# Side pieces wait for a read bank, and two transposes become pieces of their own

## The chip, the cores and the metric

The kernel runs on one core of one Trainium2 chip. The metric is the device time of one launch in microseconds (us): the median of several runs, 1270.43 us for the kernel before (three runs, 1270.27 to 1271.31).

## The reference, cut to what matters

One inference step of a decoder layer, for a prompt of 512 tokens and a sample group of 8 sequences with 4 tokens each (544 token columns in all), everything in float32. Cut down:

```python
u = rmsnorm(h)
qa, ka, va, qkv_b, z_b, beta, a, gate_a, gate_b = split(u @ w_in)
A = dilated_attention(qa, ka, va)     # 3 dilations x 4 heads x 64; the sample reads cached keys and values
B = gated_deltanet(qkv_b, z_b, beta, a)   # 8 heads x 128, convolution ahead, chunked recurrence, matrix state
h += (sigmoid(gate_a) * (A @ w_branch_a) + sigmoid(gate_b) * (B @ w_branch_b)) @ w_out
h += cross_attention(rmsnorm(h), memory)  # 256 memory tokens, 4 heads
h += (silu(conv3(n @ W_gate) + b) * (n @ W_up)) @ W_down,   n = rmsnorm(h)
y = rmsnorm(h)
```

All new caches and states are outputs too. What the change touches is the sample's part of the dilated attention: one softmax per sample row over all three dilations, and the product with the values.

## The kernel before

**Dense work.** The weights come as 128x1024 blocks, in the order of a fixed plan. Each block is loaded (`wr`), split into a high part `wh` (ScalarE copy) and a low part `wl` (VectorE subtraction), and multiplied as three products (high by high, high by low, low by high) with the 544 columns in two halves of 272. So one of the eight steps of a block is six matmuls into a wide PSUM buffer `pd`; two such buffers take turns. `u` is the normed input (`uh`, `ul`), `A` and `ob` the two branches (`Ah`, `obh`, and so on), `m` the memory tokens, `th` a gate.

**Side work.** Everything else (dilated attention, DeltaNet, softmaxes, transposes) runs in between as generators, "streams". A piece is what a stream does between two `yield`s; it usually begins with matmuls or transposes into small PSUM banks `b`, of which there are four in rotation, and ends with VectorE (DVE) or ScalarE (ACT) instructions that read them. Names: `ssc` holds the sample's scores, `so` its output, `kc` cached keys or values, `qz` and `pz` the queries and probabilities spread out, `dk`, `dq`, `sc`, `pt`, `vt` the prompt's dilated attention; `y` convolved rows, `vm` and `sz` the update of the sample's DeltaNet states, `U`, `W`, `T` the inverse of a triangular matrix, `xc`, `vn`, `St` the recurrence over chunks, `ft` and `z` tiles fetched back from DRAM.

**What sets the order.** While the program is built, an account keeps a clock for each engine, by a cost for each instruction. After every dense step `tick` (L635) goes through the streams that are runnable, by priority, and runs a piece if its inputs are ready by the account, memory slots are free, and VectorE and ScalarE do not lag too far behind. The engines then run their instructions in just that order. A piece whose `yield` says `"at", t` is ready at t. The stream `dil_sample` is marked free (`free=True`): what its pieces leave running is not counted for its readiness, only what it names with `on` or `"at"`. `acc.last` holds, for each tile, when the account has its last use done; `slot_of` keeps the list of banks in `self.ring["b"]`; `acc.done` is when the latest instruction of the piece ends. All instructions are recorded through one helper, so every row of the profile has the line L329.

Of the kernel before, what the change touches and what calls it, by code (L numbers as in the profile page):

```python
# [392 lines left out]
class Builder:  # L393
# [239 lines left out]
    def tick(self):  # L633

        c = self.clk  # L635
        t0 = c["PE"]
        self.flush()
        while c["PE"] - t0 < PE_SHARE:
            runs = self.runnable()
            for n in sorted(range(len(runs)), key=lambda n: (runs[n]["prio"], runs[n]["ready"])):  # L640
                st = runs[n]
                lag = max(c["V"], c["A"]) - c["PE"]
                if st["ready"] <= c["PE"] and self.room(st, [a + b for a, b in zip((MAIN, 0), self.older(runs, n))]) and lag < LAG[st["prio"]] and c["P"] - c["PE"] < 6.0:
                    self.step(st)
                    break
            else:
                return
# [1032 lines left out]
    def dil_sample(self):  # L1680
# [64 lines left out]
        n = 0  # L1745
# [41 lines left out]
        v.reciprocal(z, z)  # L1787
        v.tensor_scalar(sc, sc, z, None, op0=OP.mult)
        del bs
        yield 1, 0, 2, 0  # L1790
        pb = self.bank((128, 384))
        for g in range(3):
            nc.tensor.transpose(pb[:, 128 * g:128 * g + 128], sc[:, col(g):col(g) + 128], ident)
# [16 lines left out]
        for g in range(3):  # L1810
            for j in range(8 if g else 2):
# [9 lines left out]
                n += 1  # L1821
                yield
        v.tensor_tensor(o, o, acc[:, None, :].to_broadcast([128, 2, 64]), OP.add)
        yield from self.wait(("ap", 0), ("ap", 1))
        pb = self.bank((128, 128))
        nc.tensor.transpose(pb, o.rearrange("p h d -> p (h d)"), ident)
# [460 lines left out]
MAIN, PE_SHARE, LAG = 5, 2.5, {0: 4.5, 1: 2.0, 2: 2.0, 3: 1.5}  # L2287
# [52 lines left out]
```

## Time and profile before

| | |
|---|---|
| median of 3 runs | 1270.43 us |
| the profiled execution | 1269.83 us |
| its span | 1268.1 us |
| TensorE busy | 1222.2 us (96%) |
| VectorE / ScalarE / GpSimd busy | 709.4 / 526.6 / 160.9 us |
| granted TensorE clock, mean | 0.988 of full speed |

The span is the first to the last instruction; the execution has 1.7 us around it. TensorE's busy time counts overlapping matmuls once and includes slow ones, so stalls show as idle time before an instruction, in brackets with what ended it, and a lower clock shows in the windows.

### The profile page before, as it was taken

How to read it: one execution, taken by the hardware profiler on the slowest of the kernel's cores; microseconds unless marked ns; L12 is line 12 of the kernel's file. 1: busy time of each engine (PE TensorE's matmuls, PEld its weight loads, DVE VectorE, ACT ScalarE, POOL GpSimd, SP SyncE). 2: the span in 40 equal slices, each digit the busy share in tenths (PEclk: the TensorE clock that was granted, in tenths of full speed). 3: DMA queues.
4: the chain of work that ended last, by engine and by line, in shares of the span. 5: the costliest groups of instructions: out<-in, count | busy, mean ns of one | idle time of the engine just before them, and what ended most of it. 6: DMA issues, size and time to landing. Idle time of an engine off the chain costs nothing.

```text
span 1268.1 us, 25946 instructions
## 1 busy us (share of the span) xinstructions
PE 1222.2 (96%) x10482; PEld 1165.2 (92%) x10482; DVE 709.4 (56%) x1343; ACT 526.6 (42%) x1115; POOL 160.9 (13%) x356
## 2 busy tenths in 40 slices
PE   7999999999999999998999999799999999999997
PEld 6899988899999988998799998499999999999997
DVE  6535346666767974486566555364553355434564
ACT  6334434555645533665642234254332233312341
POOL 0000100211152130020000000021210022101110
PEclk9999999999999998999998999899999999999998
DMA  6332774653576568656564483545555555555422
GB/s 224 95 122 79 279 265 155 214 174 100 178 267 215 200 215 295 199 190 193 175 219 143 166 325 110 191 171 186 193 187 183 183 189 206 203 184 183 157 83 71
DMA packets 90117, 233.56 MB, mean 184 GB/s; under 512 B 25865, under 2 KB 31478, under 8 KB 89221
## 3 DMA queue, kind: packets, MB, share of 16 engines
q1 hardware_dynamic: 89998, 231.90, 53.1%
q8 instruction: 83, 1.36, 0.4%
q14 instruction: 36, 0.29, 0.1%
HBM read 198.42 MB, written 77.58 MB: 218 GB/s over the span
## 4 chain that ended last, share of the span: by engine, by line
PE 71%; DVE 5%; ACT 2%; issue 2%; DMA 1%; POOL 0%; DVEq 0%; POOLq 0%; SPq 0%; ACTq 0%
PE pd L329 58%; PE b L329 13%; DVE wl L329 1%; DVE y L329 1%; ACT wh L329 1%; DMA qk<-park 0%; DVE xr L329 0%; DMA ft<-park 0%; DVE sz L329 0%; DVE m L329 0%; DMA mvs<-in_mvs 0%; DVE st L329 0%; DMA z<-park 0%; ACT hsq L329 0%; DVE su L329 0%
## 5 line engine op out<-in xcount | busy, mean ns | idle before, releaser
L329 DVE TENSOR_TENSOR wl<-wr,wh 128x1024 fp32r<-128x1024 f32 (+2 forms) x174 | 212.4, 1223 | 225.2 <-ACT wh L329 219.1
L329 ACT ACTIVATE wh<-wr 128x1024 fp32r<-128x1024 f32 (+2 forms) x174 | 177.1, 1021 | 122.7 <-PE pd L329 120.5
L329 PE MATMUL pd<-uh,wh 128*128 128x272 f32 x1024 | 223.5, 300 | 0.0
L329 PE MATMUL pd<-ul,wh 128*128 128x272 f32 x1024 | 212.7, 289 | 0.4 <-DVE ul L329 0.3
L329 PE MATMUL pd<-uh,wl 128*128 128x272 f32 x1024 | 212.3, 288 | 0.0
L329 PEld LDWEIGHTS pd<-uh,wh 128*128 128x128 f32 x1024 | 160.2, 189 | 7.7 <-issue 6.4
L329 PEld LDWEIGHTS pd<-ul,wh 128*128 128x128 f32 x1024 | 162.1, 189 | 0.9 <-DVE ul L329 0.8
L329 PE MATMUL pd<-nh,wh 128*128 128x272 f32 x768 | 161.6, 291 | 0.5 <-DVE xr L329 0.5
L329 PEld LDWEIGHTS pd<-uh,wl 128*128 128x128 f32 x1024 | 161.8, 188 | 0.0
L329 PE MATMUL pd<-nh,wl 128*128 128x272 f32 x768 | 159.4, 288 | 0.0
L329 PE MATMUL pd<-nl,wh 128*128 128x272 f32 x768 | 159.3, 288 | 0.0
L329 PEld LDWEIGHTS pd<-nh,wh 128*128 128x128 f32 x768 | 121.9, 188 | 2.3 <-issue 2.0
L329 PEld LDWEIGHTS pd<-nl,wh 128*128 128x128 f32 x768 | 121.7, 188 | 0.0
L329 PEld LDWEIGHTS pd<-nh,wl 128*128 128x128 f32 x768 | 121.6, 188 | 0.0
L329 POOL TENSOR_TENSOR sr<-fy,rf 128x512 f32<-128x512 f32 (+1 forms) x44 | 53.5, 1237 | 69.5 <-ACT fy L329 66.3
L329 DVE SCALAR_TENSOR_TENSOR y<-cb,par,y 128x568 f32<-128x568 f32 x72 | 58.9, 820 | 2.9 <-ACT y L329 1.1
L329 PE MATMUL pd<-fh,wh 128*128 128x272 f32 x256 | 53.2, 288 | 0.0
L329 PE MATMUL pd<-fl,wh 128*128 128x272 f32 x256 | 53.1, 288 | 0.0
L329 PE MATMUL pd<-fh,wl 128*128 128x272 f32 x256 | 53.1, 288 | 0.0
L329 DVE SCALAR_TENSOR_TENSOR fy<-fcb,par,fy 128x560 f32<-128x560 f32 x44 | 35.3, 802 | 22.4 <-ACT fy L329 21.7
L329 PEld LDWEIGHTS pd<-fh,wl 128*128 128x128 f32 x256 | 40.6, 188 | 0.0
L329 PEld LDWEIGHTS pd<-fh,wh 128*128 128x128 f32 x256 | 40.5, 188 | 0.0
(371 smaller groups left out, 2121.0 us busy)
## 6 DMA issues: line engine op xcount, KB each, us to landing
wr<-in_w SPq DMA_DIRECT2D x145, 512.0 KB
out_d<-in_c SPq DMA_DIRECT2D x32, 1022.0 KB
ft<-park SPq DMA_DIRECT2D x40, 256.0 KB
kc<-in_ck SPq DMA_DIRECT2D x18, 512.0 KB
kc<-in_cv SPq DMA_DIRECT2D x18, 512.0 KB
wr<-in_wd SPq DMA_DIRECT2D x16, 512.0 KB
out_d<-in_c SPq DMA_DIRECT2D x8, 1016.0 KB
park<-y SPq DMA_DIRECT2D x24, 256.0 KB
```

The source lines that it names most:

```text
L329: return f(*a, **k)
```

## The change

`tick` asks one more thing of a stream before it runs a piece: the bank that is the fourth last in the list, the one the next piece will take first, must have been used for the last time by the account's TensorE clock. In `dil_sample`, the piece with the transposes of `ssc` is no longer ready at once behind the softmax, but when the account has the softmax done; and the final transpose of `so` likewise waits for the last addition.

```diff
-                if st["ready"] <= c["PE"] and self.room(st, [a + b for a, b in zip((MAIN, 0), self.older(runs, n))]) and lag < LAG[st["prio"]] and c["P"] - c["PE"] < 6.0:
+                if max(st["ready"], self.acc.last.get(self.ring["b"][-4], 0.0) - 0.0 if len(self.ring["b"]) >= 4 else 0.0) <= c["PE"] and self.room(st, [a + b for a, b in zip((MAIN, 0), self.older(runs, n))]) and lag < LAG[st["prio"]] and c["P"] - c["PE"] < 6.0:
                     self.step(st)
...
         v.tensor_scalar(sc, sc, z, None, op0=OP.mult)
         del bs
-        yield 1, 0, 2, 0
+        yield "at", self.acc.done, (1, 0, 2, 0)
         pb = self.bank((128, 384))
         for g in range(3):
             nc.tensor.transpose(pb[:, 128 * g:128 * g + 128], sc[:, col(g):col(g) + 128], ident)
...
         v.tensor_tensor(o, o, acc[:, None, :].to_broadcast([128, 2, 64]), OP.add)
+        yield "at", self.acc.done, (0, 0, 0, 0)
         yield from self.wait(("ap", 0), ("ap", 1))
         pb = self.bank((128, 128))
         nc.tensor.transpose(pb, o.rearrange("p h d -> p (h d)"), ident)
```

Every engine has the same number of instructions as before; their order differs from the dilated attention of the prompt (about 180 us) to the end of the branch products (about 674 us). Numbers in the rows below are buffer numbers and differ between the two programs.

TensorE before, around the transposes of the softmax's result (`ssc`): a product of the prompt's attention (`pt`, `vt`) ends, one dense step follows, then the transposes.

```order
L329 MATMUL b_2439<-pt_2412,vt_1923 64x128
L329 MATMUL b_2439<-pt_2423,vt_1923 64x128
L329 MATMUL pd_2343<-uh_409,wh_2153 128x272 x2
L329 MATMUL pd_2343<-ul_410,wh_2153 128x272 x2
L329 MATMUL pd_2343<-uh_409,wl_2154 128x272 x2
L329 MATMUL b_2466<-ident,ssc_274 128x128 x3
L329 MATMUL b_2487<-dk_1014,dq_924 128x512
```

TensorE now at the same transposes (the end of 24 rows of dense matmuls, eight steps):

```order
L329 MATMUL pd_2515<-uh_409,wh_2339 128x272 x2
L329 MATMUL pd_2515<-ul_410,wh_2339 128x272 x2
L329 MATMUL pd_2515<-uh_409,wl_2340 128x272 x2
L329 MATMUL pd_2515<-uh_419,wh_2339 128x272 x2
L329 MATMUL pd_2515<-ul_420,wh_2339 128x272 x2
L329 MATMUL pd_2515<-uh_419,wl_2340 128x272 x2
L329 MATMUL b_2566<-ident,ssc_274 128x128 x3
```

The transposes moved nine dense steps down. The final transpose of `so`, once behind a product of `kc` and `pz`, now has three dense steps between.

ScalarE before, at the first block of the memory keys and values: `m<-sso` is the root for a pair of heads, with a table load on each side of it, `th` the last gate, `wh_7786` and `wh_7828` weights of the memory blocks.

```order
L329 ACTIVATE ft_7144<-b_7753,rqs_4235 128x128
L329 ACT_TABLE_LOAD
L329 ACTIVATE m_7773<-sso_5305,eps 128x4x2
L329 ACT_TABLE_LOAD
L329 ACTIVATE th_7777<-pd_7689 128x544
L329 ACTIVATE wh_7786<-wr_7587 128x1024
L329 ACTIVATE Ah_7822<-A_971 128x544
L329 ACTIVATE wh_7828<-wr_7683 128x1024
```

ScalarE now, from the last gate on (the pair of table loads stands ahead of the gate before this one):

```order
L329 ACTIVATE th_7936<-pd_7806 128x544
L329 ACTIVATE wh_7945<-wr_7648 128x1024
L329 ACTIVATE Kd_7963<-b_7964,kd_5762 128x128 x4
L329 ACTIVATE vn_7982<-b_7980,a_5760 128x128
L329 ACTIVATE ft_7874<-b_7990,rinv_5738 128x128 x4
L329 ACTIVATE m_8004,sso_6302<-b_8001,rqs_5763 128x128
L329 ACTIVATE ft_7882<-b_8001,rqs_5763 128x128
L329 ACTIVATE ft_7907<-b_8007 32x4x32
L329 ACTIVATE Ah_8014<-A_971 128x544
L329 ACTIVATE wh_8020<-wr_7800 128x1024
```

The root and its two table loads moved up by one gate block.

TensorE before, at the last two heads of the second branch (`ident,ft` are a head's transposes; `obh_8901` and `obh_8905` are what becomes of them):

```order
L329 MATMUL pd_8816<-obh_8756,wh_8762 128x272 x2
L329 MATMUL pd_8816<-obl_8757,wh_8762 128x272 x2
L329 MATMUL pd_8816<-obh_8756,wl_8763 128x272 x2
L329 MATMUL b_8883<-ident,ft_8445 128x128 x4
L329 MATMUL b_8894<-ident,ft_8555 128x128 x4
L329 MATMUL pd_8766<-obh_8901,wh_8640 128x272 x2
L329 MATMUL pd_8766<-obl_8902,wh_8640 128x272 x2
```

TensorE now at the second of these two heads (the first one's transposes stand four dense steps further up):

```order
L329 MATMUL b_8882<-ident,ft_8474 128x128 x4
L329 MATMUL pd_8851<-obh_8704,wh_8797 128x272 x2
L329 MATMUL pd_8851<-obl_8705,wh_8797 128x272 x2
L329 MATMUL pd_8851<-obh_8704,wl_8798 128x272 x2
L329 MATMUL pd_8851<-obh_8770,wh_8797 128x272 x2
L329 MATMUL pd_8851<-obl_8771,wh_8797 128x272 x2
L329 MATMUL pd_8851<-obh_8770,wl_8798 128x272 x2
L329 MATMUL pd_8801<-obh_8901,wh_8736 128x272 x2
L329 MATMUL pd_8801<-obl_8902,wh_8736 128x272 x2
```

The two heads' transposes moved apart and up, by six and by two dense steps. The vm products of the second group stand, in both programs, at the same dense step: before, 16 products of `U` and `ft` follow the first four and 16 of `W` and `T` the second four; now four transposes follow the first four, and two products of `vn` the second four. Of the first group's vm products both stand earlier by about 40 dense steps, and one dense step later the products `qk` begin.

## Rows read from the trace of the kernel before

**Rows 1.** The page: busy time of the engines, granted clock by slice

```profile
PE 1222.2 (96%) x10482; PEld 1165.2 (92%) x10482; DVE 709.4 (56%) x1343; ACT 526.6 (42%) x1115; POOL 160.9 (13%) x356
...
PEclk9999999999999998999998999899999999999998
```

**Rows 2.** Waits of TensorE: total us, times, longest us

```profile
PE b L329 <- DVE sz L329: 2.8, 6, 0.8
...
PE b L329 <- DVE xc L329: 1.7, 2, 1.5
PE pd L329 <- ACT wh L329: 1.6, 2, 0.9
PE pd L329 <- DVE wl L329: 1.5, 2, 0.8
...
PE b L329 <- issue: 1.1, 2, 0.9
```

**Rows 3.** Timeline at ssc: start, us, engine, operation [idle before]

```profile
201.88 0.57 DVE L329 CUSTOM_DVE_ANT_0 ssc<-ssc,bs 128x390 f32<-128x390 f32 x1
...
203.62 0.42 DVE L329 TENSOR_SCALAR ssc<-ssc,m 128x390 f32<-128x390 f32 x1
...
204.19 0.52 PE L329 MATMUL b<-ident,ssc 128*128 128x128 f32 x3 [1.87 <-DVE ssc L329]
```

**Rows 4.** Timeline of TensorE at so

```profile
264.04 0.41 PE L329 MATMUL pd<-uh,wh 128*128 128x272 f32 x2
...
264.79 0.41 PE L329 MATMUL pd<-uh,wh 128*128 128x272 f32 x2
...
267.87 0.30 PE L329 MATMUL b<-ident,so 128*128 128x128 f32 x1 [0.83 <-DVE so L329]
```

**Rows 5.** Timeline of TensorE behind the first vm products

```profile
415.80 0.66 PE L329 MATMUL b<-ident,y 128*128 128x128 f32 x4 [0.83 <-DVE sz L329]
```

**Rows 6.** Timeline of TensorE behind the second group's vm products

```profile
473.77 0.22 PE L329 MATMUL b<-U,ft 32*32 32x32 f32 x2 [0.88 <-issue]
...
480.31 0.24 PE L329 MATMUL b<-W,T 32*32 32x32 f32 x2 [0.76 <-DVE sz L329]
```

**Rows 7.** Timeline of VectorE: the additions that free four banks

```profile
472.99 2.48 DVE L329 TENSOR_TENSOR sz<-sz,b 128x512 f32<-128x512 f32 x4 [1.65 <-PE b L329]
```

**Rows 8.** Windows: us, busy by engine, granted clock, DMA share, GB/s

```profile
475.98:479.39 3.41, 3.41 (x14) 1.79 (x14) 1.40 (x4) 0.23 (x1) 0.00 (x0) 0.50 1.14 330
482.81:486.22 3.41, 3.36 (x48) 2.83 (x48) 0.28 (x1) 2.09 (x7) 0.00 (x0) 0.50 1.03 417
588.62:592.03 3.41, 3.41 (x22) 3.39 (x16) 2.48 (x8) 0.65 (x2) 0.00 (x0) 0.50 0.96 323
667.13:673.96 6.83, 5.55 (x25) 5.07 (x23) 4.13 (x6) 1.71 (x2) 0.00 (x0) 0.50 0.30 116
```

**Rows 9.** Timeline of ScalarE, then TensorE, at the first memory block

```profile
580.41 1.28 ACT L329 ACT_TABLE_LOAD   x1
...
582.02 1.28 ACT L329 ACT_TABLE_LOAD   x1
583.32 0.62 ACT L329 ACTIVATE th<-pd 128x544 f32<-128x544 f32 x1
...
584.94 0.39 PE L329 MATMUL pd<-mh,wh 128*128 128x256 f32 x1 [0.94 <-ACT wh L329]
```

**Rows 10.** Timeline at the last two heads: fetch, its reader, TensorE

```profile
662.10 0.86 SPq L329 DMA_DIRECT2D z<-park  x2
...
665.05 0.75 DVE L329 SCALAR_TENSOR_TENSOR z<-b,par,z 128x512 f32<-128x512 f32 x1 [1.28 <-DMA z<-park]
...
666.22 0.92 PE L329 MATMUL b<-ident,ft 128*128 128x128 f32 x4 [2.03 <-DVE ft L329]
...
668.77 0.82 PE L329 MATMUL pd<-obl,wh 128*128 128x272 f32 x2 [1.28 <-DVE obl L329]
```

**Rows 11.** Waits of SP's DMA queue, the longest

```profile
SPq L329 <- DVE wl L329: 524.2, 103, 17.0
```

## The prediction

> **What bounds the kernel now.** I read the page first: TensorE is busy for 96% of the span [rows 1], and in the chain of waits its own matmuls make up most of the path. So a change in the order of TensorE's work is worth what TensorE itself stands still, or runs slowly, and nothing else. The waits of TensorE alone come next [rows 2]: they are short, some 1 to 3 us in total by releaser, and each has a place. I then looked each place up in the timeline [rows 3 to 7, 9, 10], and last asked the windows what clock was granted just behind them [rows 8]. The reader is to see three kinds of loss in the part that the change reorders (about 180 to 674 us): a side piece put before its input is there [rows 3, 4], a side piece put before the small bank it needs is free [rows 5, 6], and the tail of the stage, where weights or the last two heads come late [rows 9, 10]. [...]
>
> **The pace that hides things.** One dense step is six matmuls; two steps start at 264.04 and 264.79, so it takes 0.75 us [rows 4]. Whatever chain is shorter than the dense steps now standing over it costs nothing.
>
> **The change part by part.** Up to the dilated prompt piece at about 180 us both programs have the same order, so that stretch counts zero. Behind that, term by term, against the profiled execution of 1269.83 us:
>
> (a) The two new "at" pieces. Before, the three transposes of ssc stand behind the matmuls of one step, and TensorE idles 1.87 us for the softmax, whose first instruction starts at 201.88 and whose last starts at 203.62 and takes 0.42: 2.2 us in all [rows 3]. In the new order 24 rows of dense matmuls, eight steps or 6.0 us, stand right ahead of them, so the whole chain is covered. The transpose of so idles 0.83 us for the vector additions right ahead of it [rows 4]; in the new order three steps (2.25 us) stand between. Both go: -2.7. The products that read the copy of ssc's transposes stand 16 steps further on, so nothing is late in their place. Were the second still late, -1.9.
>
> (b) The bank rule at the first four vm products (state update of the sample, at about 413 us): the transposes of y, one dense step behind them, idle 0.83 us [rows 5]. In the new order the qk products again stand one step behind the four. The four vector additions that free the banks take 2.48 us together [rows 7], one every 0.62. I count 0; bounds -0.83 and +0.83 (qk takes two banks, and the rule looks at the oldest alone).
>
> (c) The second group's four vm products, twice. Before, U products come right behind, without a dense step, and W products behind the second four. All idles on sz and the unnamed ones ("issue") are 2.8 + 1.1 us [rows 2]; without the 0.83 of (b) 3.1 us lie here [rows 6]. In the new order one set of transposes, which needs one bank, follows the first four, then a dense step; two chain products, a bank each, follow the second four. By the rows that is 0.88 once more, and 0.88 plus one 0.33 (the next addition): 2.1 of 3.1 stay, -1.0. The clock is at 0.50 for 3.41 us twice around here [rows 8]; TensorE was busy all through, so each costs up to 3.41 / 2 = 1.7. I count one of the two as gone, -1.7 (bounds 0 and -3.4). The idles ahead of the first fall in that clock are 0.88 us at most, and the new order keeps such idles, which speaks against counting both. [...]
>
> (d) The recurrence's product (xc, U): TensorE waited for xc 1.7 us in all, 1.5 of it at one place [rows 2]. The recurrence stands 6 to 20 steps earlier in the new order, with other neighbours; nothing says whether it meets the same queue. Bounds 0 and -1.7, value -0.85.
>
> (e) The memory keys and values. Here a block of weights lasts a few microseconds, and TensorE waits 1.6 us for wh and 1.5 us for wl, twice each [rows 2]. The first pair has its cause in ScalarE's row: two table loads of 1.28 us stand directly ahead of the gate's th and the wh that is wanted at 584.94 [rows 9]. In the new order these loads stand one whole gate block (eight steps, 6.0 us) earlier, with another gate's th and wh between, where 2.6 us of loads are covered. So half of the 3.1 goes by this, and of the other half I take half: -2.3 (bounds -1.5 and -3.1). The fall of the clock behind it, 3.41 us from 588.62 [rows 8], I count half: -0.85. The second load ends at 583.30 and th starts at 583.32, so a load costs its 1.28 us and no more [rows 9]. [...]
>
> (f) The tail. The last heads' recurrence ended so late that the two sets of transposes of the last heads stand side by side, directly ahead of the matmuls that read them. The fetch of z is issued at 662.10, its reader starts at 665.05, TensorE idles 2.03 us and then 1.28 us for obl [rows 10], and the clock is 0.50 from 667.13 to 673.96 [rows 8]. In the new order the recurrence's last products stand 11 dense steps (8 us) earlier, one set of transposes stands six steps and the other two steps ahead of the first matmul that reads them. The whole path from the last transposes to obl took 668.77 - 666.22 = 2.55 us; two steps, and one more before the second head is read, cover 2.25. So 0.3 of 3.31 stays: -3.0. The slow stretch is 6.83 us with 1.28 idle in it: (6.83 - 1.28) / 2 = 2.8 comes back. -5.8 together; bounds -3.3 (the clock falls all the same) and -6.1.
>
> (g) What it adds. I count 134 changes from side work to dense work against 128 in this stretch; at 0.1 us each 0.6. The fetches that the pieces issue move with them on SP's queue, past loads of weights; that queue mostly stands waiting for a weight buffer to come free, 524 us of the span [rows 11], so a place in it is not scarce. And the moved pieces meet new neighbours: before, TensorE lost 1.7 us on xc and 0.83 at the vm products in places that nothing in the code forbids. I take as much again, 2.5 us, in new waits; bounds 0 and 6.
>
> Sum: -2.7 + 0 - 1.0 - 1.7 - 0.85 - 2.3 - 0.85 - 5.8 + 0.6 + 2.5 = -12.1. 1269.83 - 12.1 = 1257.7. The median of the runs shown is 0.6 above the profiled execution, so 1258.3 in the terms of the metric.
>
> **Rivals.**
> Only the direct part comes. The reordering moves waits about and finds as many new ones, and just (a) is left: 1270.43 - 2.7 = 1267.7. For it speaks that a bank wait is only a small part of TensorE's loss (2.8 us on sz, [rows 2]), so the rule as such can save little, and that (c) to (f) come from where pieces happen to land. Against it: (e) and (f) have their cause in one order of rows each, and both rows are visibly moved.
>
> Everything comes. All idles of (a), (c) to (f) and all four slow stretches go, no new ones: 2.7 + 3.1 + 3.4 + 1.7 + 3.1 + 1.7 + 3.3 + 2.8 = 21.8, 1248.6 us. For it: the later stage is now ahead of its need throughout. Against: (c) shows waits that stay.
>
> Slower: held pieces bunch up, and a piece that takes two or four banks waits for those that the rule doesn't look at. Its place is the dilated attention and the products with cached values, which stand up to 36 steps later and in longer unbroken runs (38 matmuls between two dense steps at the longest). The price is the 0.88 us that follows four unread banks [rows 6], and with it a slow stretch of 1.7 each [rows 8]. It decides once the gains of (c) to (f) are used up: with (a) and half of (f), 5.6 us, kept, four such places with their slow stretches cost 10.3 and leave +4.7: 1275. Against it: in the first third of the span the clock row shows no fall [rows 1], although side pieces follow each other there too.
>
> **Chances.** Forecast (1254 to 1264) 0.58; everything comes (under 1254) 0.14; only the direct part (1264 to 1270) 0.20; slower 0.08. The first two and most of the third lie below 1267.9, that is faster by over 0.2%, about what a measurement of this kernel can tell from no change: 0.84. Within 0.2% (to 1273): 0.11. Slower: 0.05. The range is 1250 to 1268: below it lies a part of "everything comes", above it the slower case and a little of the third.
>
> **What would show it.** In the new profile the rows "PE b <- DVE ssc" and "PE b <- DVE so" are gone (a). Behind the second group's vm products an idle of about 0.9 stands ahead of transposes and of vn products (c). No wait for wh at the first memory block (e). At the last two heads no idle over 0.5 and a clock of 1.00 (f); the stretch from the first obh matmul to the last is then 6 us shorter. Row PEclk has fewer 8s in the middle. It is wrong if new idles over 1 us appear between 200 and 330 us, where the held pieces went, or if the tail still waits for obl.

## The result, and the profile after

The changed kernel takes 1261.16 us (median of 4 runs, 1261.06 to 1262.31) against 1270.37 (4 runs, 1270.27 to 1271.31): ratio 0.9928, 95% interval 0.9911 to 0.9945. In a second series the same order of instructions took 1263.92 against 1269.87, ratio 0.9948 (0.9933 to 0.9962). So the change gains 6 to 9 us. The forecast was 1258.3 with a range of 1250 to 1268.

The profiled execution took 1261.06 us, 8.8 less than that of before. The windows say in which stage; below each kernel's four, before first: the input projections with all the side work, the memory block with the attention's output projection, the output projection of the recurrence, and the cross attention (columns as in [rows 8]; the seventh number is the granted clock).

```profile
32.73:580.97 548.24, 537.79 (x5079) 506.31 (x5078) 336.31 (x771) 264.62 (x668) 85.69 (x208) 0.99 0.57 189
580.97:652.38 71.41, 66.84 (x641) 59.60 (x640) 44.74 (x101) 43.71 (x123) 0.00 (x0) 0.98 0.68 225
652.38:710.62 58.24, 54.93 (x413) 53.96 (x412) 32.98 (x52) 16.65 (x27) 0.00 (x0) 0.94 0.42 142
759.26:825.44 66.18, 57.74 (x400) 42.77 (x399) 29.80 (x66) 22.69 (x62) 1.77 (x4) 0.95 0.45 166
```

```profile
31.36:584.50 553.14, 543.76 (x5203) 511.92 (x5202) 346.76 (x794) 268.99 (x681) 87.42 (x208) 0.99 0.57 191
584.50:652.17 67.67, 63.90 (x535) 58.84 (x534) 39.50 (x85) 41.94 (x119) 0.00 (x0) 0.95 0.62 211
652.17:703.49 51.32, 49.95 (x393) 49.65 (x393) 31.07 (x47) 13.75 (x18) 0.00 (x0) 1.00 0.47 158
752.13:816.72 64.59, 56.13 (x400) 43.08 (x399) 29.80 (x66) 22.67 (x62) 1.76 (x4) 0.97 0.45 170
```

The reader is to see where TensorE's own pieces went, too: 124 more of the recorded matmuls stand in the first stage (5203 against 5079) and 106 and 20 fewer in the next two, and so in part the first stage is 4.9 us longer and the next two 3.7 and 6.9 shorter. TensorE's idle time (the stretch less TensorE's busy time) fell in all three, by 1.1, 0.8 and 1.9 us; the time at half clock stayed at 6.8 us in the first, rose from 3.4 to 6.8 in the second and fell from 6.8 to 0 in the third. Together the three stages are 5.8 us shorter.

The other 3.0 us lie where both programs have the same order: 1.4 in the start, up to 32.73 and 31.36, and 1.6 in the cross attention, where the clock fell for two stretches before and for one after. The start is chance: in the fourteen profiles of this document it ended anywhere from 31.4 to 34.7. Of the cross attention that isn't shown. It took 64.6 to 65.0 us in all six profiles with the changed kernel's last heads and no or one edit ahead of them, and 66.2 to 67.7 in the six where the last heads wait for ft and obl; but two orders without these waits (all_later and best below) took 66.2 and 67.4. So the change's own part of this profile is 5.8 us, or 7.4 if the cross attention hangs on it; the second series lies between, at 6.0 by the medians and 6.6 by the ratio.

On the page, against [rows 1], TensorE is busy 4.2 us less with the same number of matmuls. The slow stretches explain up to 3.4 of it, an estimate, half of what they are shorter: 17.1 us in all, outside the end of the kernel, against 23.9.

```profile
PE 1218.0 (97%) x10482; PEld 1165.6 (93%) x10482; DVE 712.6 (57%) x1343; ACT 526.4 (42%) x1115; POOL 162.5 (13%) x356
...
PEclk9999999999999999999999999999999999999998
```

TensorE's waits, against [rows 2]: ssc, so, xc and wh have no row any more, sz fell from 2.8 to 1.0. Against that, y is new, and m and St have grown from 0.5 and 0.4; the last row here is what is left of sz.

```profile
PE b L329 <- DVE m L329: 2.9, 2, 2.5
PE b L329 <- DVE St L329: 2.9, 1, 2.9
...
PE b L329 <- DVE y L329: 2.0, 1, 2.0
...
PE b L329 <- DVE sz L329: 1.0, 2, 0.7
```

The timeline of TensorE in the changed kernel has their places: the transposes of y, what is left of the second group [rows 6], the state St of the recurrence, the spread of the memory block's scale, and one wait in the last heads, where [rows 10] had two.

```profile
365.29 1.08 PE L329 MATMUL b<-ident,y 128*128 128x128 f32 x4 [2.00 <-DVE y L329]
...
476.66 0.66 PE L329 MATMUL b<-ident,ft 128*128 128x128 f32 x4 [0.28 <-DVE sz L329]
480.86 0.49 PE L329 MATMUL b<-vn,Kd 128*128 128x128 f32 x2 [0.70 <-DVE sz L329]
...
555.48 0.49 PE L329 MATMUL b<-St,ft 128*128 128x128 f32 x2 [2.90 <-DVE St L329]
...
594.15 1.22 PE L329 MATMUL b<-ident,m 128*128 128x128 f32 x4 [2.52 <-DVE m L329]
...
666.96 0.49 PE L329 MATMUL pd<-obh,wh 128*128 128x272 f32 x2 [1.37 <-DVE ft L329]
```

Three of these have a stretch at half the clock (0.50) beside them. They take the place of the four of [rows 8].

```profile
365.17:368.58 3.41, 3.29 (x16) 3.32 (x17) 3.41 (x4) 1.14 (x8) 1.98 (x3) 0.50 0.90 300
556.32:559.73 3.41, 3.41 (x18) 3.41 (x17) 3.27 (x10) 0.00 (x0) 0.52 (x1) 0.50 0.00 0
593.86:600.69 6.83, 6.54 (x54) 5.96 (x55) 2.14 (x6) 2.20 (x9) 0.00 (x0) 0.50 0.29 94
```

### The profile page after: what moved, and what is told of

It is laid out like the page before. It is cut to its first block, busy times and chain, and to the rows that moved or that the text cites. A ratio compares the mean times of both kernels' runs of the same rounds, so it can differ in the third digit from the quotient of the medians.

```text
span 1259.3 us, 25957 instructions
## 1 busy us (share of the span) xinstructions
PE 1218.0 (97%) x10482; PEld 1165.6 (93%) x10482; DVE 712.6 (57%) x1343; ACT 526.4 (42%) x1115; POOL 162.5 (13%) x356
## 4 chain that ended last, share of the span: by engine, by line
PE 86%; DVE 6%; ACT 3%; DMA 2%; issue 2%; SPq 1%; POOL 0%; POOLq 0%; DVEq 0%; ACTq 0%
PE pd L329 68%; PE b L329 17%; DVE wl L329 1%; ACT wh L329 1%; SPq L329 1%; DMA kc<-in_cv 0%; DVE u L329 0%; DMA x<-in_xT 0%; DMA U<-usol 0%; DVE xr L329 0%; DVE y L329 0%; DVE ml L329 0%; DVE ul L329 0%; DVE st L329 0%; DMA ft<-park 0%
```

## The experiments

My theory was that the gain is the direct part (a) plus what happens to land well, above all the tail (f); the rival, that the bank rule itself saves the stalls. Single edits to this planner move everything behind them, so for most runs the order of the changed kernel was written down as a table, "at this dense step run these pieces", and the planner's choice replaced by a look into it; then a line of the table can be edited and the rest stays. The names in it are the pieces (dil_sample0 is the dilated sample, gdn_chain the recurrence of one pair of heads, gdn_final3 the outputs of the last two heads). Each of the twelve was timed beside the kernel before, on one of three chips; its median there was 1269.5 to 1270.7, so runs of different chips are compared by the ratio to before. after_again, y_later, rstd_later and all_later are one series on one chip. The last column of the table is the mean of time multiplied by granted clock over the runs: by estimate what would be left at full clock throughout, so it separates what TensorE stood still from what it ran slowly. The clock is on record to 0.001, which is 1.3 us of this product, so smaller differences in it mean little.

```
                              median us   range              ratio to before (95%)      clock   time x clock
before (46 runs)               1270.2    1267.0 to 1272.4        1                      0.987   1253.3
changed (first series)         1261.16   1261.06 to 1262.31   0.9928 (0.9911 to 0.9945) 0.990   1249.1
after_again                    1263.92   1261.29 to 1265.46   0.9948 (0.9933 to 0.9962) 0.989   1249.7
rule_only                      1280.36   1277.91 to 1282.89   1.0080 (1.0067 to 1.0092) 0.982   1257.2
ats_only                       1277.33   1275.78 to 1279.76   1.0055 (1.0043 to 1.0067) 0.987   1260.7
slack_m05                      1283.11   1281.40 to 1283.93   1.0100 (1.0085 to 1.0115) 0.982   1259.4
slack_p03                      1263.71   1261.20 to 1264.38   0.9943 (0.9930 to 0.9957) 0.992   1252.7
tail_undone                    1273.76   1269.88 to 1274.41   1.0020 (1.0011 to 1.0029) 0.987   1256.2
transposes_back                1265.86   1262.72 to 1268.65   0.9966 (0.9953 to 0.9978) 0.990   1253.1
y_later                        1261.40   1259.37 to 1264.08   0.9936 (0.9921 to 0.9951) 0.990   1248.9
rstd_later                     1258.84   1257.73 to 1259.74   0.9910 (0.9895 to 0.9925) 0.993   1250.0
all_later                      1259.53   1256.38 to 1260.99   0.9914 (0.9898 to 0.9930) 0.991   1248.5
scale_out                      1257.86   1257.17 to 1261.56   0.9911 (0.9897 to 0.9924) 0.990   1246.0
best                           1259.17   1256.96 to 1261.43   0.9916 (0.9902 to 0.9930) 0.992   1249.2
```

**The rule alone.**

```diff
-        yield "at", self.acc.done, (1, 0, 2, 0)
+        yield 1, 0, 2, 0
...
-        yield "at", self.acc.done, (0, 0, 0, 0)
```

> The bank rule alone, without the two transposes as pieces of their own. Theory (the tail's gain needs the whole reordering, the rule by itself only moves waits about): in this program's order the last two heads' eight transposes stand together behind the whole output projection of the heads again, as before, so the 5.8 us of the tail don't come, and the 2.7 us of the two transposes don't come either: 1268 to 1272. Rival (the rule is what saves the stalls): all of the gain but the 2.7 us, 1264.

It took 1280.36, 9.7 us more than before and worse than either theory said. The rival falls. The place is the last part of the first stage: three waits follow each other, and the clock is low for 23.89 us, from behind the first of them to 5 us past the last.

```profile
570.78 0.49 PE L329 MATMUL b<-St,ft 128*128 128x128 f32 x2 [1.02 <-DVE St L329]
574.20 0.45 PE L329 MATMUL b<-ident,so 128*128 128x128 f32 x1 [2.93 <-DVE so L329]
...
590.53 0.77 PE L329 MATMUL b<-vn,Kd 128*128 128x128 f32 x2 [2.25 <-DVE U L329]
```

```profile
572.14:596.03 23.89, 19.36 (x165) 16.06 (x166) 15.34 (x38) 11.80 (x37) 6.31 (x9) 0.50 0.66 201
```

**The two transposes alone.**

```diff
-                if max(st["ready"], self.acc.last.get(self.ring["b"][-4], 0.0) - 0.0 if len(self.ring["b"]) >= 4 else 0.0) <= c["PE"] and ...
+                if st["ready"] <= c["PE"] and ...
```

> The two transposes as pieces of their own, without the bank rule. Theory: the direct part, 2.7 us, comes (1.9 at the first, 0.8 at the second), the tail stands as before: 1267.7, between 1266 and 1270. Rival (the reordering that any one-step shift sets off is what gains): 1261 to 1264. Rival (nothing of the direct part is left, because a later wait takes it up): 1270.

It took 1277.33, 6.6 us more than before; all three expectations fall. The two waits of (a) are gone, so the direct part came and was lost again further on: at y and at the banks of the sample's state updates, and in the tail, which is 1.8 us longer than in the kernel before, with the waits of [rows 10].

```profile
366.12 0.63 PE L329 MATMUL b<-ident,y 128*128 128x128 f32 x4 [2.00 <-DVE y L329]
382.02 1.16 PE L329 MATMUL b<-qk 128*128 128x128 f32 x8 [0.85 <-DVE sz L329]
...
670.95 1.11 PE L329 MATMUL b<-ident,ft 128*128 128x128 f32 x4 [1.95 <-DVE ft L329]
673.70 0.82 PE L329 MATMUL pd<-obl,wh 128*128 128x272 f32 x2 [1.19 <-DVE obl L329]
```

So one part costs 9.7 us, the other 6.6, and both together gain 6 to 9. They don't add: each decides the whole order behind it.

**The tail put back.** The table's lines of gdn_chain6, gdn_chain7, gdn_final2 and gdn_final3 from step 548 on are those of the kernel before, up to 13 steps later.

```diff
-    576: "gdn_final2 gdn_chain7 gdn_final3",
-    578: "gdn_final3 gdn_final3 gdn_final3",
...
+    587: "gdn_chain7 gdn_final3",
+    588: "gdn_final3 gdn_final3 gdn_final3",
```

> The changed kernel with its order kept everywhere but in the last two heads of the second half: the steps of the chain, of the preparation of their outputs and the transposes stand where the kernel before had them, so the last eight transposes stand together behind the projection. Theory (step f of the sum): the two idles (3.3 us) and the slow clock behind them (2.5 to 2.8 us) come back: 1267.0. Rival (the clock's part is lost elsewhere anyway): 1264.5. Rival (the tail's waits were covered): 1261.2.

It took 1273.76, 9.8 us more than after_again (9.1 by the ratio) where 5.8 were expected. The waits of [rows 10] are back almost to the number, with the low clock at the second, for 3.41 us where it was 6.83. Another came that the kernel before didn't have: a fetch of ft inside the attention's output projection, since the chain's late steps now stand there. By the stages of the two profiles the tail is 6.8 us longer than in after_again (58.1 against 51.3), as in the kernel before; the cross attention, with the same order, is 2.9 longer.

```profile
636.53 0.49 PE L329 MATMUL b<-vn,ft 128*128 128x128 f32 x2 [2.24 <-DMA ft<-park]
...
666.78 0.92 PE L329 MATMUL b<-ident,ft 128*128 128x128 f32 x4 [1.93 <-DVE ft L329]
...
669.34 0.82 PE L329 MATMUL pd<-obl,wh 128*128 128x272 f32 x2 [1.39 <-DVE obl L329]
```

**The two transposes put back, the order kept.**

```diff
-    184: "dil_sample0 dil_prompt1 dil_prompt1",
-    192: "dil_sample0",
+    184: "dil_sample0 dil_sample0 dil_prompt1 dil_prompt1",
...
-    258: "dil_sample0 dil_sample0",
-    261: "dil_sample0 dil_sample0",
+    258: "dil_sample0 dil_sample0 dil_sample0 dil_sample0",
```

> The changed kernel with its order kept, but the transposes of the dilated scores and of the dilated output put back right behind the VectorE work that feeds them, as before. Theory (step a): TensorE waits there again, 1.9 us at the first and 0.8 at the second: 1263.9. If a slow stretch of the clock follows the 1.9, 1265.6. Rival (TensorE was idle there for something that is late anyway, so the wait only moves): 1261.2.

1265.86: 1.9 us more than after_again, 2.3 by the ratio, where the two intervals overlap. The two waits are back, 2.8 us together where (a) had 2.7, and no low clock behind them. So (a) is worth 2 to 3 us, as forecast: the waits show it, the times agree but would not show it alone.

```profile
201.70 0.52 PE L329 MATMUL b<-ident,ssc 128*128 128x128 f32 x3 [1.28 <-DVE ssc L329]
...
285.77 0.30 PE L329 MATMUL b<-ident,so 128*128 128x128 f32 x1 [1.51 <-DVE so L329]
```

**The new waits, one by one.** First the changed kernel itself from its table (no edit), then the y pieces and the memory scale moved alone, then both with the St piece.

> The changed kernel itself, with its order written down in a table in place of being worked out: the order is the same, so this is the point from which the next three are read. Every theory: 1261 to 1264. If the 9 us of the change hang on where the clock happens to fall in single executions, the runs spread over more than 5 us and the median comes nearer to the kernel before, 1265.

> The changed kernel with one group of pieces (the transposes of y, the second product m, and the two qk products at 365 us) three dense steps later, the rest of the order kept. Theory (TensorE waits 2.0 us there because VectorE is slow, and a stretch at half clock follows): the wait and the stretch go, -2.0 and -1.7: 1257.5. Rival (the wait only moves to the next piece of the chain that hangs on m): 1259.5 to 1261.

```diff
-    347: "conv16 gdn_sample0 gdn_group0 gdn_group0",
+    350: "conv16 gdn_sample0 gdn_group0 gdn_group0",
```

> The changed kernel with the spread of the memory block's scale put at its seventh instead of its fourth step (k == 6 for k == 3), the rest of the order kept. Theory (the wait of 2.5 us behind the table load, and the 6.8 us at half clock that cost 3.4, are owed to that place): 1255.3. If only the idle goes and the slow stretch stays: 1258.7. Rival (the pieces that then stand ahead of it wait for the same ScalarE row): 1261.

```diff
-                if h == 1 and k == 3:
+                if h == 1 and k == 6:
```

> The changed kernel with both of these and the St piece at 555 us two dense steps later, ahead of the splits of the memory rows on VectorE. Theory (the new waits of the changed kernel, 2.0, 2.9 and 2.5 us, with three slow stretches, 1.7, 1.7 and 3.4, are what holds it back): -13 to -14, 1248. Rival (each place has another wait behind it): 1255 to 1258.

```diff
     (both of the above, and)
-    512: "mem_stream0 mem_stream0 gdn_chain3",
-    514: "gdn_solve1",
+    514: "gdn_chain3 gdn_solve1",
+    515: "mem_stream0 mem_stream0",
```

after_again: 1263.92, as expected; its runs spread over 4.2 us, and each run's time goes with its clock (1261.29 at 0.991, 1265.46 at 0.988). Its profile has the order of the changed kernel and not its slow stretches: none behind St, where the wait is 2.3 us, and 10.24 us at the memory block in place of 6.83. y_later: 1261.40, -2.5, between theory and rival, but by the ratio only 1.5 and within the noise. The wait of 2.00 is gone; the products of the sample's chain behind it now begin one step behind the group instead of four, and the second of them waits 1.35.

```profile
371.64 0.49 PE L329 MATMUL b<-m,m 128*128 128x128 f32 x2 [1.35 <-ACT m L329]
```

rstd_later: 1258.84, -5.1, where the theory said -5.9 from its 1261.2. The memory block is 4.9 us shorter than in after_again's profile (64.6 against 69.4). By time x clock the two are the same: of the 2.52 us of idle 1.56 are still there, in three small waits, and what was gained is the time at half clock, which is gone.

```profile
595.36 0.66 PE L329 MATMUL b<-ident,ft 128*128 128x128 f32 x4 [0.82 <-ACT m L329]
596.63 0.82 PE L329 MATMUL b<-W,T 32*32 32x32 f32 x16 [0.39 <-DVE W L329]
...
599.38 0.39 PE L329 MATMUL pd<-mh,wh 128*128 128x256 f32 x1 [0.35 <-DVE mkT L329]
```

all_later: 1259.53, no better than rstd_later alone. The theory's 1248 falls; the rival holds in kind, though its 1255 to 1258 was too low: with St put off, the product behind it waits instead.

```profile
558.41 0.49 PE L329 MATMUL b<-xc,U 128*128 128x128 f32 x2 [1.53 <-DVE xc L329]
```

**VectorE beside GpSimd.**

```diff
-            nc.gpsimd.tensor_tensor(s0[hh], s0[hh], self.eGs[...][:, :, None].to_broadcast([128, 8, 128]), OP.mult)
+            if g:
+                nc.gpsimd.tensor_tensor(s0[hh], s0[hh], self.eGs[...][:, :, None].to_broadcast([128, 8, 128]), OP.mult)
```

> The changed kernel, order kept, without the scaling of the first group's four states by the gates on GpSimd (8.45 us from 356.1; the output of the samples lacks that factor). Theory (VectorE's instructions are drawn out while GpSimd runs its tensor_tensor, and that is why y comes 2.0 us late at 365): with GpSimd still, the three y and the Dm at 354.6 to 361 take 2.2 and 0.7 us instead of 4.0 and 2.4, the wait of 2.0 us at 365 and the slow stretch behind it go, 1260.2 from the 1263.9 of the same kernel with the scaling. Rival (VectorE is late because of its own queue, whatever GpSimd does): the durations stay, 1263.9.

1257.86: -6.1 by the medians of two chips, -4.7 by the ratio, where -3.7 was expected. The rival falls. The timeline of the changed kernel, VectorE and then GpSimd:

```profile
354.61 4.01 DVE L329 SCALAR_TENSOR_TENSOR y<-cb,par,y 128x568 f32<-128x568 f32 x3
358.55 2.38 DVE L329 TENSOR_TENSOR Dm<-Gb,const 128x512 f32<-128x512 f32 x1
361.40 1.23 DVE L329 SCALAR_TENSOR_TENSOR qk<-b,br,Dm 128x128 f32<-128x128 f32 x4 [0.47 <-ACT Dm L329]
...
363.58 3.30 DVE L329 SCALAR_TENSOR_TENSOR y<-th,y 128x568 f32<-128x568 f32 x2
...
356.09 8.45 POOL L329 TENSOR_TENSOR sz<-sz,eGs 128x1024 f32<-128x1024 f32 x4 [5.50 <-PE b L329]
```

The same instructions of VectorE without the scaling, and TensorE's transposes of y, which now wait for nothing:

```profile
356.08 2.49 DVE L329 SCALAR_TENSOR_TENSOR y<-cb,par,y 128x568 f32<-128x568 f32 x3
358.49 0.69 DVE L329 TENSOR_TENSOR Dm<-Gb,const 128x512 f32<-128x512 f32 x1
359.65 1.23 DVE L329 SCALAR_TENSOR_TENSOR qk<-b,br,Dm 128x128 f32<-128x128 f32 x4 [0.47 <-ACT Dm L329]
...
361.83 1.83 DVE L329 SCALAR_TENSOR_TENSOR y<-th,y 128x568 f32<-128x568 f32 x2
...
364.60 0.60 PE L329 MATMUL b<-ident,y 128*128 128x128 f32 x4
```

4.01 becomes 2.49, 2.38 becomes 0.69, 3.30 becomes 1.83: 4.7 us of VectorE's row, of which the planner's account knows nothing. The stages give the gain its places: against after_again's profile the first stage is 3.5 us shorter, about as expected, and the memory block 3.1, since the clock is low there for 3.41 us instead of 10.24. As the changed kernel itself had 6.83 there once and 10.24 once, that second part may be chance.

**Other margins in the rule.**

```diff
-                if max(st["ready"], self.acc.last.get(self.ring["b"][-4], 0.0) - 0.0 if ...
+                if max(st["ready"], self.acc.last.get(self.ring["b"][-4], 0.0) + 0.3 if ...
```

> The changed kernel with a margin of 0.3 us in the bank rule (a piece begins 0.3 us after the oldest bank has been read by the account, not at that moment). Theory (what counts is where pieces land, not that banks are free): in this order the last eight transposes stand together behind the projection again, so the tail's idles come back and other places gain or lose a few us each: 1268 to 1278. Rival (the rule itself saves the stalls, and 0.3 us more of it changes little): 1261 to 1265.

> The changed kernel with a margin of -0.5 us in the bank rule (a piece may begin 0.5 us before the oldest bank has been read by the account). With margins of 0 and 0.3 us the time was the same, 1263.9 and 1263.7, though the waits stood in other places. Theory (what counts is where pieces land; that two orders gave the same sum is chance): anything from 1260 to 1278, with the tail's idles back, as the last eight transposes stand together here too. Rival (rule and separate transposes together give about 6 us at any small margin, since the sum of waits is less): 1262 to 1266.

(The second has "- 0.5" there.) With +0.3 the time is 1263.71, the rival's number, and my theory's number falls. But the trace shows another kernel: the tail is as bad as before,

```profile
660.25 0.92 PE L329 MATMUL b<-ident,ft 128*128 128x128 f32 x4 [2.08 <-DVE ft L329]
662.80 0.82 PE L329 MATMUL pd<-obl,wh 128*128 128x272 f32 x2 [1.38 <-DVE obl L329]
```

and made up for elsewhere. The three stages of the result section take 670.7 us together against 672.1, with 14.0 us of idle against 14.5, and the clock is low in them for 6.83 us, all of it in the tail, against 13.65. (The first stage alone is 10 us shorter, but 88 of its recorded matmuls have moved to the next two.) With -0.5 it is 1283.11, the slowest of all and outside both expectations, with waits of 2.0 us for sz and 2.6 for m and a clock that stays low for 20.48 us.

```profile
573.99:594.47 20.48, 17.45 (x188) 14.45 (x189) 13.88 (x36) 12.64 (x41) 7.59 (x11) 0.50 0.38 126
```

Half a microsecond in the margin moves the time by 19 us; that is what speaks for "where pieces land". That two margins, 0 and 0.3, both gain about 6 us speaks for the rule together with the separate transposes. Two orders don't settle it, and it stays open.

**A version that beats both.**

```diff
     (the scale at k == 6, St and the memory rows as in the run with all, and)
-    347: "conv16 gdn_sample0 gdn_group0 gdn_group0",
+    347: "gdn_sample0 gdn_group0 gdn_group0",
+    350: "conv16",
...
-    516: "gdn_chain3 mem_stream0",
+    516: "mem_stream0",
+    518: "gdn_chain3",
```

> The changed kernel with three places moved in its order: the spread of the memory block's scale three steps later, as in the run before with that alone; the transposes of y at 365 us three dense steps later, without the pieces behind them; the St piece at 555 us two dense steps later with the rest of its chain, ahead of the memory rows on VectorE. Theory (each of the three new waits and the slow stretch behind it goes, and with room behind the moved pieces no next wait takes its place): from 1258.8 with the first of them, -2.0 and -2.3 of idle and up to 3.4 of clock: 1251 to 1254. Rival (as when all were moved at once: others wait in their stead): 1258 to 1260.

1259.17, the rival's value. In its profile the first stage is 2.7 us shorter than in rstd_later's, and the cross attention, where nothing was moved, 2.5 longer, with the clock low for 10.24 us against 3.41; one profile of each doesn't show whether that is chance. Two waits of the kind it was to remove stand at other pieces:

```profile
375.17 0.49 PE L329 MATMUL b<-m,m 128*128 128x128 f32 x2 [2.37 <-ACT m L329]
...
567.16 0.49 PE L329 MATMUL b<-xc,U 128*128 128x128 f32 x2 [1.46 <-DVE xc L329]
```

The first waits for ScalarE's m, which stands behind rows that wait for Dm, and Dm is late behind the y (3.32 us for two, where the changed kernel's took 3.30 beside GpSimd and scale_out's 1.83): moving the piece didn't touch the cause. So the best version that leaves nothing out is rstd_later, one number in the code with the order held by the table: 1258.84, against 1263.92 for the changed kernel in the same series, and 0.9910 of before; all_later and best (0.9914 and 0.9916) can't be told from it.

## Why the prediction was right, and where it was not

The number was right, 1261.16 and 1263.92 against 1258.3, and in part by luck. The working forecast a gain of 12.1 us; the profile has 8.8, and of these only 5.8 lie in the stages whose order the change touches. Old waits and slow stretches went nearly as in the rival "everything comes", about 20 of its 21.8 us, and new ones took most of that back. So the working was right in the steps that had a cause in single rows, and wrong in the one that had none.

(a) Forecast -2.7. Both rows are gone; put back alone, 2.8 us of wait returned and the median rose by 1.9 (2.3 by the ratio). Right.

(b) Forecast 0 (bounds ±0.83). The wait of [rows 5] is gone: -0.8.

(c) Forecast -1.0 of idle and one slow stretch of two. Of 3.1 us 0.98 are left (0.28 and 0.70), and both stretches at 476 and 483 us are gone. I had kept more waits than there are, and had taken the idles that stay as a reason against counting both. Here idles of 0.28 and 0.70 us remain and the clock stays at 1.00 from 472.57 to 489.63 us: the reason didn't hold.

(d) Forecast -0.85, half of xc's 1.7. xc is gone, but the same recurrence now waits 2.9 us for St and is followed by a slow stretch. The neighbour that I couldn't name is the split of the memory rows (ml), which stands ahead of St on VectorE. It is drawn out, as y is: two of them take 1.86 us while GpSimd adds up macc (553.29, 1.59 us for two), and 0.88 when it doesn't; the st and su of 550.58 take 0.8 us each beside the macc before that, where their like takes 0.28. That is some 2 of the 2.9 us, by the lengths of the rows; no run took the macc out.

```profile
553.31 1.86 DVE L329 SCALAR_TENSOR_TENSOR ml<-mem,par,mh 128x256 fp32r<-128x256 f32 x2
...
556.88 0.88 DVE L329 SCALAR_TENSOR_TENSOR ml<-mem,par,mh 128x256 fp32r<-128x256 f32 x2
```

(e) Forecast -3.15. The waits for wh and wl fell from 3.1 to 0.43 there, more than the 2.3 forecast, and the slow stretch of 588 us is gone; the two table loads do stand earlier, at 568 and 576. What failed is that I took two table loads for all of them: a third comes with the memory block's scale. Before, it ran at 586.39, just as TensorE began the sum for it (586.42, behind its waits for wh and wl), and side pieces and the slow stretch lay between that and the scale's transposes at 590.09. Now the sum runs at 589.86 and the load at 592.35, behind ft, Ah and a wh, and TensorE is ready for the transposes 0.7 us before the load begins.

```profile
592.35 1.28 ACT L329 ACT_TABLE_LOAD   x1
593.64 0.26 ACT L329 ACTIVATE m<-b,eps 128x2 f32<-128x2 f32 x1
```

That one place gave back all of (e): 2.5 us of wait and 6.83 at half the clock. rstd_later shows it: moved from there, the scale costs 1.56 us of waits and no low clock.

(f) Forecast -5.8: 3.0 of waits and 2.8 of clock. The clock's part came, 1.00 over the stage. The two waits of [rows 10] are gone, but an obh product of the last heads waits 1.37 us for ft, where I had 0.3 left and no idle over 0.5: so 1.9 us of waits went, and 4.7 in all. The stage is 6.9 us shorter, as some 20 matmuls have left it too. Right in kind and 1.1 too large. That the tail undone costs more, 9.8, doesn't show it too small: that order has waits in the attention's projection that the kernel before hadn't, and a longer cross attention. That the tail falls well is no work of either part: alone, neither moved it.

(g) This is the step that failed: 2.5 us for new waits, bounds 0 to 6. The new waits are 2.0, 2.9, 2.5 and 1.4 us and eight of 0.2 to 0.6, 12 in all, and the three slow stretches, 13.65 us at 0.50, lose up to another 6.8 by my estimate: 19, not 2.5. The 0.1 us for a change from side to dense work agrees with the trace of before: two dense matmuls right behind side work take 0.52 us (247.40), the next two 0.41 (247.76). Part of it was made up for by what I had left standing, (b), the rest of (c) to (e) and some small waits, and in the total by 3.0 us at the start and in the cross attention, which I had counted at nothing. I took the price of new neighbours from the two that before had lost most by; a planner that places some 640 pieces makes new ones everywhere.

The rival "only the direct part comes" had the better description of the mechanism (waits move about, as many new ones as old), but not its number, since by luck or not the tail came too. "Everything comes" had the old losses right and failed in "no new ones". The rival "slower" was off in its place: no wait over 0.5 us stands between 200 and 330 us. It lies close all the same: each half of the change is slower by itself, and in both the new profile has new waits, as in (g).

## What to carry to other kernels

Where a planner lays out work by its own account of costs, a small rule is a new draw of the whole order: read its gain from the waits in the new trace, not from the wait that it was to remove, and try each part alone before crediting it. Price the new neighbours by how many pieces move, look for what the account leaves out (here VectorE drawn out beside GpSimd, 4.7 us of its row; it does count a table load, at 1.3 us where the trace has 1.28), and for work that stands at a fixed step of the dense work whatever the planner does (here the memory block's scale, with the third table load). Then fix the waits at the row that causes them: moving the piece that waits, as with y and St, only handed the wait on.

## What the runs showed of the hardware

Three of VectorE's rows took longer while GpSimd ran its tensor_tensor, up to 3.4 times: Dm<-Gb,const 2.38 us against 0.69 without the scaling, y<-cb,par,y 1.34 against 0.83 each, y<-th,y 1.65 against 0.92 each. Of qk<-b,br,Dm, with one input in a bank, four took 1.23 us both times. That the GpSimd work is the cause is shown for these rows, by taking it out; for ml ahead of St it is read from two rows alone (1.86 against 0.88 us for two). GpSimd's own four scalings took 8.45 us here.

Much of the spread between runs of one order goes with the clock: after_again took 1261.29 us at 0.991 and 1265.46 at 0.988, the kernel before 1267.02 at 0.991 and 1272.43 at 0.985. Of each gain in the table 3 to 8 us go with it, an estimate by time against time x clock. Before and after, the cross attention has the same order and the same waits within 0.1 us, and yet ran 1.6 us apart (66.18 and 64.59), with two slow stretches and with one. Over the profiles its clock is low for 3.41 us (the changed kernel), 6.83 (before) or 10.24 (tail_undone) with the same instructions. Whether a wait draws the clock down isn't settled by these runs: behind St it fell after 2.90 us in the changed kernel's profile, and not after 2.3 in after_again's.
